# Moving the low parts of 60 weight blocks, the row gathers and half of the gates: a transformer kernel with product-key experts on one Trainium2 core

## The chip, the cores and the metric

The program runs on one core of a Trainium2 chip. The metric is the device time of one execution in microseconds. A core has five engines that run their own instruction streams in order and wait for each other through semaphores: TensorE (PE, matrix products, with its weight loads shown as PEld), VectorE (DVE), ScalarE (ACT), GpSimd (POOL) and SyncE (SP, which here issues most DMAs). Sixteen DMA engines move data; their requests come from SP's queue (q1 in the profile) and from POOL's (q0).

## What is computed

Two transformer blocks follow each other on one sequence of 512 tokens of width 1024, in float32. The first has differential attention, a pooling branch, a gated convolution and a gated feed-forward layer of width 2816. The second has three attention branches and then a feed-forward layer made of 16,384 experts, of which each token takes 128 (8 heads, 16 each). The change is about the last one, and about the feed-forward layer of the first block:

```python
def peer_ffn(h, w_q, keys1, keys2, u, v):
    q = (h @ w_q).reshape(B, S, PEER_HEADS, 2, half)
    s1 = jnp.einsum('bshd,hkd->bshk', q[..., 0, :], keys1)
    s2 = jnp.einsum('bshd,hkd->bshk', q[..., 1, :], keys2)
    v1, i1 = lax.top_k(s1, PEER_TOPK)
    v2, i2 = lax.top_k(s2, PEER_TOPK)
    cand = v1[..., :, None] + v2[..., None, :]           # 16 x 16 per head
    sv, si = lax.top_k(cand.reshape(..., 256), PEER_TOPK)
    e1 = jnp.take_along_axis(i1, si // PEER_TOPK, axis=-1)
    e2 = jnp.take_along_axis(i2, si % PEER_TOPK, axis=-1)
    experts, gates = e1 * N_KEYS + e2, jax.nn.softmax(sv, axis=-1)
    # per token: a = u[experts] . h ; out = (gelu(a) * gates) . v[experts]
```

## The kernel before

**Products in three parts.** A float32 product is made of three TensorE products: each operand is split into a high part (ScalarE copies it to float32r) and a low part (VectorE subtracts the high part from the whole), and high x high, low x high and high x low are added in PSUM (`product`, lines 394 to 396). Weights come in a fixed order as blocks of 128 x 1024 (512 KB). `Stream` loads a block on SP's queue into one of four raw buffers (`wr`), ScalarE makes `wh` (line 81) and, after `LAG` = 2 ticks, VectorE makes `wl` (line 83; through the counting wrapper `Counted` it shows as line 189). Three buffers of each are there, and up to two split blocks are kept ahead of the one in use.

**An order written out by hand.** Instructions are put in order by the Python program. After each three-part product (`gemm` calls it) comes a tick: `Later.tick` lets every waiting generator run its next step, and at last calls `fill`. `Balance` is the plan: a count of TensorE's columns (`pe`), and of VectorE's estimated work in the same unit (`dve`). `behind()` is the difference, and `room()` makes a generator wait while it is over 2000. A 384-column three-part product counts 3 x 396 = 1188, a VectorE instruction on 1024 float32 columns 2746. Nothing in the plan counts ScalarE or DMA.

**Stages.** The first block's feed-forward layer is three groups of w_gate_up and w_down blocks. Much later come the expert layer's stages:
- *Selection.* w_peer_q products and scores; `select` finds the top 16 on VectorE for three token groups of 128 (0 to 2) and, in a chain of its own, for the fourth (3).
- *u stage.* Tokens 0 to 383 (`ND`) go through all 16,384 experts as dense products: 128 u blocks, 24 TensorE instructions each. `ev_u` writes the Gelu of a block on ScalarE (line 1805) to one of two buffers `full`, and SP stores it in DRAM (`a_d`, 192 KB).
- *Gates.* Beside the u stage `gates` makes a dense gate matrix from the selection, in 48 groups of 8 tokens: VectorE makes two one-hot matrices (`oh1`, `oh2h`) and two products of one of them with the high and low part of the gate values (`ogh`), TensorE multiplies them (line 1709), ScalarE evicts to `stg` (line 1713), and SP stores in `g_d`.
- *v stage.* 128 v blocks. `fetch` reads Gelu and gate for eight blocks from DRAM into `ag`, `activate` multiplies them on VectorE, one block at a time and one block ahead, and splits the result (line 1797 and VectorE); lines 1863 to 1865 add all into eight PSUM banks.
- *Rows.* Tokens 384 to 511 take their own 128 experts each: 128 gathers of u rows and 128 of v rows (line 1642, an indirect DMA of 512 KB on POOL's queue into one of four buffers `ub`), each followed by one VectorE instruction of 1024 columns. `one_by_one` does one and asks for the gather four later. `fill` calls it at the end of a tick if `behind()` is under 800; v rows only in the v stage.

Of the kernel before, what the change touches and what calls it, by code (L numbers as in the profile page):

```python
# [22 lines left out]
D = 1024  # L23
# [21 lines left out]
NUB = 4  # L45


class Stream:
# [7 lines left out]
    def __init__(self, nc, raw, parts, entries, on_raw, later):  # L56
        self.nc, self.raw, self.parts, self.entries, self.on_raw = nc, raw, parts, entries, on_raw
        self.later = later
# [7 lines left out]
    def load(self):  # L66
        while self.loaded < len(self.entries) and self.loaded < self.done + self.RAW:
            key, ap, n, split = self.entries[self.loaded]
            t = self.raw.tile([128, 1024], F32, name="wr")
            self.nc.sync.dma_start(t[:, :n], ap)  # L70
            self.r[self.loaded] = t
            self.loaded += 1

    def _one(self):
# [14 lines left out]
        self.load()  # L89

# [68 lines left out]
class Balance:  # L159
# [3 lines left out]
    def __init__(self):  # L163
        self.pe = self.dve = 0.0
# [7 lines left out]
    def behind(self):  # L172
        return self.dve - self.pe

# [34 lines left out]
def tile_kernel(ctx, tc, a, out):  # L209
# [51 lines left out]
    ents(seq_ff, 1, range(40, 48))  # L261
# [11 lines left out]
    dr = ctx.enter_context(tc.tile_pool(name="dr", bufs=1, space=bass.MemoryType.DRAM))  # L273
    ph1 = ExitStack()
# [25 lines left out]
    stream = Stream(nc, wraw, wpart, entries, mod_chunk, later)  # L300
# [715 lines left out]
    with tc.tile_pool(name="ffp", bufs=2) as ffp:  # L1016
        for g, (f0, f1) in enumerate(FGROUPS):
# [444 lines left out]
    stream.low = dv  # L1462
    a_d = dr.tile([32, 128, 4, ND], F32, name="a_d")
# [89 lines left out]
    def select(t0, nt, big):  # L1553
# [5 lines left out]
        for h in HEADS:  # L1559
# [9 lines left out]
            cand, ixr, oneh = big()  # L1569
# [4 lines left out]
            for i in range(2):  # L1574
                for t in range(nt):
                    nc.scalar.activation(ixr[:, i, t], ixf[:, i, t, :, None].to_broadcast([128, 16, 16]), AF.Copy)
# [419 lines left out]
```

## Time and profile before

| | us |
|---|---|
| median of 3 runs | 2498.8 (2495.02 to 2503.24) |
| the profiled execution | 2499.26 |
| its span, first to last instruction | 2497.5 |
| TensorE busy in it | 2384.8 (95%) |
| VectorE busy | 1854.5 (74%) |
| ScalarE busy | 1081.7 (43%) |
| POOL busy | 456.4 (18%) |
| mean granted TensorE clock | 0.989 |

The page gives busy times and shares of the whole span, and then the span in 40 slices of 62 us. A share over the whole span is a mean over stages with different limits; so the table of stretches, the waits and the instructions in order of time are read for the places of interest. A tile's name in a row is that of the program (`wl<-wr,wh` is made from `wr` and `wh`); `x46` is a count. The feed-forward stage lies at about 390 to 700 us, the u stage at 1327 to 1938, the gates within it at 1585 to 1843, and the v stage at 1945 to 2488.

### The profile page before, as it was taken

The numbers are of one execution on the slowest core, as the hardware profiler recorded it, in microseconds if no ns is written. First come the engines' busy times: TensorE is split into PE (matmuls) and PEld (weight loads), VectorE is DVE, ScalarE is ACT, GpSimd is POOL, SyncE is SP. The second block draws the span as 40 slices with busy tenths as digits, with TensorE's granted clock in tenths as the row PEclk, the third lists the DMA queues.
The fourth block names the chain that finished last, engine by engine and source line by source line (L and its number), as shares of the span: only waits on it lengthen the run. The fifth ranks groups of instructions, "written<-read, shape, count | busy, mean of one in ns | idle before, by whom it ended". The sixth has DMA issues, their size and how long they took to land.

```text
span 2497.5 us, 35741 instructions
## 1 busy us (share of the span) xinstructions
PE 2384.8 (95%) x13075; PEld 2128.1 (85%) x13075; DVE 1854.5 (74%) x3722; ACT 1081.7 (43%) x1812; POOL 456.4 (18%) x434
## 2 busy tenths in 40 slices
PE   4899999999989999999999999999987899999998
PEld 2677788888868888777889999999987899999998
DVE  7678763333567776655699999988876889999994
ACT  3566332222445555533445444566642333333332
POOL 5310000000011100000000000111224444455440
PEclk9999999999999999999999999999998999999999
DMA  6973652222256643134325555689899999999993
GB/s 243 228 209 105 217 178 101 93 101 93 85 162 158 159 123 110 51 110 148 106 86 173 183 174 174 224 323 324 336 336 405 327 402 405 404 403 404 402 401 121
DMA packets 184511, 548.94 MB, mean 220 GB/s; under 512 B 22464, under 2 KB 59072, under 8 KB 183952
## 3 DMA queue, kind: packets, MB, share of 16 engines
q1 hardware_dynamic: 132720, 381.00, 42.7%
q0 software_dynamic: 51040, 165.04, 19.8%
q8 instruction: 103, 1.69, 0.3%
q14 instruction: 72, 0.59, 0.1%
q10 hardware_dynamic: 576, 0.62, 0.1%
HBM read 478.00 MB, written 68.71 MB: 219 GB/s over the span
## 4 chain that ended last, share of the span: by engine, by line
PE 77%; DMA 8%; issue 6%; DVE 5%; ACT 2%; POOL 1%; SPq 0%; DVEq 0%; ACTq 0%; POOLq 0%
PE pg L394 17%; PE pg L396 17%; PE pg L395 17%; PE pv L1864 6%; PE pv L1863 6%; PE pv L1865 6%; DMA a_d<-full 2%; DMA ub<-in_v,idx 2%; PE pt L602 1%; DMA ub<-in_u_rows,idx 1%; PE ps L1709 1%; DVE ada L297 1%; POOL ub L1642 1%; PE po L624 1%; DMA wr<-in_v 1%
## 5 line engine op out<-in xcount | busy, mean ns | idle before, releaser
L394 PE MATMUL pg<-hh,wh 128*128 128x512 f32 (+1 forms) x2088 | 792.4, 380 | 33.2 <-ACT full L1805 19.5
L395 PE MATMUL pg<-hl,wh 128*128 128x512 f32 (+1 forms) x2088 | 765.0, 366 | 9.2 <-POOL hl L508 8.9
L396 PE MATMUL pg<-hh,wl 128*128 128x512 f32 (+1 forms) x2088 | 765.6, 367 | 3.3 <-DVE wl L189 2.6
L81 ACT ACTIVATE wh<-wr 128x1024 fp32r<-128x1024 f32 (+2 forms) x446 | 465.7, 1045 | 411.7 <-PE pv L1864 268.2
L394 PEld LDWEIGHTS pg<-hh,wh 128*128 128x128 f32 x2088 | 397.2, 190 | 75.7 <-ACT full L1805 22.8
L396 PEld LDWEIGHTS pg<-hh,wl 128*128 128x128 f32 x2088 | 396.0, 190 | 48.8 <-DVE wl L189 3.6
L395 PEld LDWEIGHTS pg<-hl,wh 128*128 128x128 f32 x2088 | 397.3, 190 | 44.8 <-POOL hl L508 11.8
L189 DVE TENSOR_TENSOR wl<-wr,wh 128x1024 fp32r<-128x1024 f32 x270 | 329.6, 1221 | 90.1 <-ACT wh L81 89.2
L1863 PE MATMUL pv<-og,wh 128*128 128x384 f32 x1024 | 345.3, 337 | 7.0 <-ACT og L1797 7.0
L1864 PE MATMUL pv<-og,wh 128*128 128x384 f32 x1024 | 346.5, 338 | 3.0 <-DVE og L189 3.0
L1865 PE MATMUL pv<-og,wl 128*128 128x384 f32 x1024 | 345.1, 337 | 0.0
L83 DVE TENSOR_TENSOR wl<-wr,wh 128x1024 fp32r<-128x1024 f32 (+2 forms) x175 | 208.1, 1191 | 111.9 <-ACT wh L81 110.1
L1642 POOL DMA_INDIRECT ub<-in_u_rows,idx x128 | 151.1, 1180 | 706.5 <-DVE dots L189 514.2
L1642 POOL DMA_INDIRECT ub<-in_v,idx x128 | 183.1, 1431 | 179.6 <-DVE rows_o L189 161.8
L1863 PEld LDWEIGHTS pv<-og,wh 128*128 128x128 f32 x1024 | 192.9, 188 | 7.4 <-ACT og L1797 7.3
L1864 PEld LDWEIGHTS pv<-og,wh 128*128 128x128 f32 x1024 | 192.8, 188 | 6.7 <-DVE og L189 6.6
L1865 PEld LDWEIGHTS pv<-og,wl 128*128 128x128 f32 x1024 | 192.8, 188 | 0.0
L1805 ACT ACTIVATE full<-pg 128x384 f32<-128x384 f32 x128 | 63.0, 492 | 284.5 <-issue 142.6
L189 DVE CUSTOM_DVE_ANT_0 ub<-ub,rows_h 128x1024 f32<-128x1024 f32 x128 | 155.6, 1220 | 29.2 <-DMA ub<-in_u_rows,idx 29.1
L189 DVE SCALAR_TENSOR_TENSOR rows_o<-ub,dots,rows_o 128x1024 f32<-128x1024 f32 x127 | 162.4, 1279 | 11.9 <-DMA ub<-in_v,idx 11.5
L1713 ACT ACTIVATE stg<-ps 128x512 f32<-128x512 f32 x96 | 105.3, 1120 | 22.3 <-PE ps L1709 22.3
L1797 ACT ACTIVATE og<-ag 128x384 fp32r<-128x384 f32 x128 | 65.9, 515 | 32.5 <-DVE ag L189 28.7
(390 smaller groups left out, 3223.8 us busy)
## 6 DMA issues: line engine op xcount, KB each, us to landing
wr<-in_u SPq DMA_DIRECT2D x128, 512.0 KB, 4.7
wr<-in_v SPq DMA_DIRECT2D x128, 512.0 KB, 10.2
wr<-in_w_in SPq DMA_DIRECT2D x66, 512.0 KB, 3.4
a_d<-full SPq DMA_DIRECT2D x128, 192.0 KB, 3.4
g_d<-stg SPq DMA_DIRECT2D x32, 768.0 KB, 9.8
ag<-a_d SPq DMA_DIRECT2D x32, 768.0 KB, 9.6
ag<-g_d SPq DMA_DIRECT2D x32, 768.0 KB, 16.0
wr<-in_w_gate_up SPq DMA_DIRECT2D x44, 512.0 KB, 3.3
```

Source lines behind the costliest of these rows:

```text
L81: self.nc.scalar.activation(hi[:, :n], t[:, :n], AF.Copy)
L83: self.low.tensor_tensor(lo[:, :n], t[:, :n], hi[:, :n].bitcast(F32), op=OP.subtract)
L189: return f(*args, **kw)
L394: nc.tensor.matmul(ps[:m, :n], w[0][:, wk], rh, start=first, stop=False)
L395: nc.tensor.matmul(ps[:m, :n], w[0][:, wk], rl, start=False, stop=False)
L396: nc.tensor.matmul(ps[:m, :n], w[1][:, wk], rh, start=False, stop=last)
L1642: nc.gpsimd.indirect_dma_start(out=got[n], out_offset=None, in_=flat[what], in_offset=bass.IndirectOffsetOnAxis(ap=idx[:, s:s + 1], axis=0))
L1713: nc.scalar.activation(stg[:, :, k0:k0 + 4].rearrange("p e t -> p t e"), pg.rearrange("p (t e) -> p t e", t=4), AF.Copy, scale=1.0 / GS)
L1797: nc.scalar.activation(hi, la, AF.Copy)
L1863: nc.tensor.matmul(ps, wh[:, c], hi, start=b == 0, stop=False)
L1864: nc.tensor.matmul(ps, wh[:, c], lo, start=False, stop=False)
L1865: nc.tensor.matmul(ps, wl[:, c], hi, start=False, stop=b == 127)
```

## The change

- **Low parts.** While the feed-forward stage runs, entries `("pre", k)` for u blocks 0 to 59 are put between its weights: the block is loaded, split, and its low part is written to DRAM (`made`) on POOL's queue. In the u stage the low part of these blocks is loaded from there on POOL's queue instead of made on VectorE.
- **Rows.** The plan also counts DMA (`transfer`, `queued`). `fill` may take a row with up to 4000 behind while fewer than 0.95 rows per block since their start are done, and none with over 5000 units of DMA queued; in the v stage rows are spread evenly over 124 blocks.
- **Gates.** The product with the low part of the gate values goes from VectorE to ScalarE, one token (128 columns, every second element) at a time.
- **Blocks two at a time.** `activate` gates two blocks in one go, two blocks ahead; the first two are gated before the u stage is over; fetches come two blocks earlier.
- **Smaller ones.** The last sums of `select` are a tree of additions; `LAG` is 4 in the expert stages; every third Gelu has a buffer of its own (`au`).

```diff
@@ -43,6 +43,8 @@
+NPRE = 60
+RATE = 0.95
...
@@ -68,6 +70,7 @@
+            self.bal.transfer(n)
...
@@ -79,14 +82,31 @@
             self.nc.scalar.activation(hi[:, :n], t[:, :n], AF.Copy)
+            if not self.ready_made(key, lo):
+                yield self.LAG
+                self.low.tensor_tensor(lo[:, :n], t[:, :n], hi[:, :n].bitcast(F32), op=OP.subtract)
+            self.p[i] = (hi, lo)
+        elif key[0] == "pre":
+            hi = self.spare.tile([128, 1024], F32R, name="ph")
+            lo = self.spare.tile([128, 1024], F32R, name="pl")
+            self.nc.scalar.activation(hi, t, AF.Copy)
             yield self.LAG
-            self.low.tensor_tensor(lo[:, :n], t[:, :n], hi[:, :n].bitcast(F32), op=OP.subtract)
-            self.p[i] = (hi, lo)
+            self.low.tensor_tensor(lo, t, hi.bitcast(F32), op=OP.subtract)
+            yield 1
+            self.nc.gpsimd.dma_start(self.made[key[1]], lo)
         else:
...
         self.load()
+    def ready_made(self, key, lo):
+        if key[0] != "u" or key[1] >= NPRE:
+            return False
+        self.nc.gpsimd.dma_start(lo, self.made[key[1]])
+        self.bal.transfer(D)
+        return True
...
@@ -171,6 +191,13 @@
+    def transfer(self, n):
+        self.dma = max(self.dma, self.pe) + 2.88 * n
+    def queued(self):
+        return self.dma - self.pe
...
@@ -237,12 +264,14 @@
-    def ents(seq, every=None, extra=()):
+    def ents(seq, every=None, extra=(), ahead=0):
...
+            if 0 <= k - 4 < ahead:
+                entries.append((("pre", k - 4), a["u"][k - 4], D, False))
...
@@ -258,7 +287,7 @@
-    ents(seq_ff, 1, range(40, 48))
+    ents(seq_ff, 1, range(40, 48), NPRE)
...
@@ -1460,6 +1493,7 @@
+    stream.LAG = 4
...
@@ -1584,16 +1618,20 @@
+            dv.tensor_tensor(oneh, sab.rearrange("p i t k -> p (i t) k")[:, :, None, :].to_broadcast(
+                [128, 2 * nt, 16, 16]), iota16[:, None].to_broadcast([128, 2 * nt, 16, 16]), op=OP.is_equal)
+            yield from room()
...
-                dv.tensor_tensor(oneh[i], sab[:, i, :, None, :].to_broadcast(sq4),
-                                 iota16[:, None].to_broadcast(sq4), op=OP.is_equal)
+                part = oneh[:, nt * i:nt * i + nt]
+                dv.tensor_tensor(part, part, ixr[i], op=OP.mult)
...
-            for i in range(2):
-                dv.tensor_tensor(oneh[i], oneh[i], ixr[:, i], op=OP.mult)
+            for n in (8, 4, 2):
+                dv.tensor_tensor(oneh[:, :, :n], oneh[:, :, :n], oneh[:, :, n:2 * n], op=OP.add)
...
-                dv.reduce_sum(dst[:, ts, h, :], oneh[i].rearrange("p t j k -> p t k j"), axis=AX)
-                yield from room()
+                dv.tensor_tensor(dst[:, ts, h, :], oneh[:, nt * i:nt * i + nt, 0], oneh[:, nt * i:nt * i + nt, 1],
+                                 op=OP.add)
+            yield from room()
...
@@ -1689,7 +1725,12 @@
         stage["pe"] = bal.pe
-        if bal.behind() < 800:
+        soon = "out" not in stage and stage["at"] < RATE * (stage.get("blk", 0) - stage.get("go", 0))
+        if "out" in stage:
+            first = stage.setdefault("first", stage["at"])
+            if stage["at"] > first + (stage["blk"] + 1) * (len(jobs) - first) / 124:
+                return
+        if bal.behind() < (4000 if soon else 800) and bal.queued() < 5000:
             one_by_one()
...
@@ -1743,9 +1784,13 @@
-            for r in range(2):
-                dv.tensor_tensor(og[:, r], oh1, of(gp[:, r, tk]), op=OP.mult)
-                yield from room()
+            dv.tensor_tensor(og[:, 0], oh1, of(gp[:, tk]), op=OP.mult)
+            yield from room()
+            for n in range(TG):
+                nc.scalar.activation(og[:, 1, n // 2, :, n % 2], oh1[:, n // 2, :, n % 2], AF.Copy,
+                                     scale=gT[:, tk.start + n:tk.start + n + 1])
+                if n % 4 == 3:
+                    yield 1
...
@@ -1760,11 +1805,13 @@
+            bal.transfer(32 * NG)
...
+            later.spawn(activate(0), 2)
...
@@ -1787,23 +1836,30 @@
             t = AG[b // 8]
-            la = t[:, 0, b % 8]
-            lav = la.rearrange("p (s t) -> p s t", s=8)
-            lg = t[:, 1, :, NG * (b % 8):NG * (b % 8) + NG]
+            two = [128, 2, ND]
+            la = t[:, 0, b % 8:b % 8 + 2]
+            lav = la.rearrange("p b (s t) -> p b s t", t=NG)
+            lg = t[:, 1, :, NG * (b % 8):NG * (b % 8) + 2 * NG].rearrange("p s (b t) -> p b s t", t=NG)
             dv.tensor_tensor(lav, lav, lg, op=OP.mult)
             yield 2
-            parts = w3.tile([128, 2048], BF, name="og").bitcast(F32R)
-            hi, lo = parts[:, :ND], parts[:, 512:512 + ND]
+            if b % 4:
+                parts = hp.tile([128, 4, ND], F32R, name="parts", tag="hl")
+                hi, lo = parts[:, :2], parts[:, 2:]
+            else:
+                hi, lo = (w3.tile([128, 1024], F32R, name="part", tag="og")[:, :2 * ND].rearrange(
+                    "p (b t) -> p b t", b=2) for i in range(2))
             nc.scalar.activation(hi, la, AF.Copy)
-            yield 2
+            yield 3
             dv.tensor_tensor(lo, la, hi.bitcast(F32), op=OP.subtract)
-            AC[b] = (hi, lo)
+            for i in range(2):
+                AC[b + i] = hi[:, i], lo[:, i]
...
         def f(ps):
-            t = tmp.tile([128, 512], F32, name="full")[:, :ND]
+            t = w3.tile([128, ND], F32, name="au", bufs=1) if b % 3 == 2 else tmp.tile([128, 512], F32, name="full")[:, :ND]
             nc.scalar.activation(t, ps, AF.Gelu)
             nc.sync.dma_start(a_d[b // 4, :, b % 4], t)
+            bal.transfer(ND)
         return f
...
@@ -1848,13 +1904,13 @@
     rows_o = hp.tile([128, 4, KD, 128], F32, name="rows_o", tag="hh")[:, 0]
-    stage["out"] = rows_o
-    for _ in activate(0):
-        pass
+    stage.update(out=rows_o, blk=0)
     for b in range(128):
-        if b % 8 == 7:
+        stage["blk"] = b
+        if b % 8 == 5:
             later.spawn(fetch(b // 8 + 2))
-        later.spawn(activate(b + 1))
+        if b % 2 == 0:
+            later.spawn(activate(b + 2))
         wh, wl = stream.get(("v", b))
```

## Rows read from the trace of the kernel before

**Rows 1.** The page's 40 slices of the span, busy tenths of TensorE.

```profile
PE   4899999999989999999999999999987899999998
```

**Rows 2.** Stretches: us, each engine's busy us (count), PEclk, DMA share, GB/s.

```profile
390.00:700.00 310.00, 309.37 (x1357) 251.40 (x1356) 123.06 (x137) 89.36 (x114) 0.54 (x1) 1.00 0.28 95
1358.00:1585.00 227.00, 227.00 (x1311) 226.77 (x1310) 215.06 (x672) 95.53 (x157) 7.34 (x6) 1.00 0.55 187
1585.00:1843.00 258.00, 258.00 (x1965) 242.84 (x1964) 227.95 (x328) 171.24 (x198) 46.88 (x43) 1.00 0.87 312
1843.00:1945.00 102.00, 72.95 (x363) 68.81 (x361) 63.35 (x92) 22.44 (x32) 45.05 (x38) 0.91 1.01 394
1945.00:2440.00 495.00, 491.79 (x2798) 488.00 (x2799) 452.69 (x571) 178.10 (x236) 234.93 (x170) 1.00 1.01 394
```

**Rows 3.** ScalarE in order of time, end of u: start, us, what, idle before.

```profile
1847.62 0.49 ACT L1805 ACTIVATE full<-pg 128x384 f32<-128x384 f32 x1 [2.72 <-issue]
1848.01 1.05 ACT L81 ACTIVATE wh<-wr 128x1024 fp32r<-128x1024 f32 x1
1851.78 0.49 ACT L1805 ACTIVATE full<-pg 128x384 f32<-128x384 f32 x1 [2.72 <-PE pg L396]
1861.93 0.49 ACT L1805 ACTIVATE full<-pg 128x384 f32<-128x384 f32 x1 [8.72 <-DMA a_d<-full]
...
1940.89 0.49 ACT L1805 ACTIVATE full<-pg 128x384 f32<-128x384 f32 x1 [0.32 <-DMA a_d<-full]
```

**Rows 4.** ScalarE's waits 1845 to 1946: total us, times, longest.

```profile
ACT full L1805 <- DMA a_d<-full: 70.4, 13, 9.0
```

**Rows 5.** DMA issues, KB, median us to landing: 1840:1945; last row 1600:1840.

```profile
wr<-in_u SPq DMA_DIRECT2D x10, 512.0 KB, 9.5
a_d<-full SPq DMA_DIRECT2D x16, 192.0 KB, 11.2
ub<-in_u_rows,idx POOLq DMA_INDIRECT x38, 8.3
...
wr<-in_u SPq DMA_DIRECT2D x46, 512.0 KB, 6.2
```

**Rows 6.** VectorE's groups from 1945 on: busy us, mean ns, idle before.

```profile
L189 DVE CUSTOM_DVE_ANT_0 ub<-ub,rows_h 128x1024 f32<-128x1024 f32 x45 | 54.8, 1218 | 1.4 <-DMA ub<-in_u_rows,idx 1.4
```

**Rows 7.** Lines 1805 and 1863: ns min/median/max, first and last start.

```profile
L1805 ACT ACTIVATE full<-pg x128: 491/492/550, 1327.4 to 1940.9; 128x384 f32<-128x384 f32 x128
...
L1863 PE MATMUL pv<-og,wh x1024: 332/337/687, 1945.2 to 2487.9; 128*128 128x384 f32 x171
```

**Rows 8.** TensorE's waits from 1945 on.

```profile
PE pv L1863 <- ACT og L1797: 7.0, 1, 7.0
PE pv L1864 <- DVE og L189: 3.0, 5, 1.2
```

**Rows 9.** POOL in order of time: the fourth gather.

```profile
1379.94 1.65 POOL L1642 DMA_INDIRECT ub<-in_u_rows,idx  x1 [16.80 <-DVE tif L189]
```

**Rows 10.** VectorE's groups 1600 to 1840.

```profile
L189 DVE TENSOR_TENSOR ogh<-oh,gp 128x1024 f16<-128x1024 f16 x88 | 56.9, 687 | 1.1
L189 DVE TENSOR_TENSOR wl<-wr,wh 128x1024 fp32r<-128x1024 f32 x46 | 56.3, 1223 | 16.5 <-ACT wh L81 16.1 <-DMA a_d<-full 0.3
```

**Rows 11.** ScalarE in order of time: four scaled copies, six copies, evictions.

```profile
1313.29 1.15 ACT L1525 ACTIVATE scs<-ps,rt 128x128 f32<-128x128 f32 x4
...
1380.51 1.93 ACT L1576 ACTIVATE og<-tif 128x256 bf16<-128x256 f32 x6
...
1838.98 1.07 ACT L81 ACTIVATE wh<-wr 128x1024 fp32r<-128x1024 f32 x1
1839.95 3.04 ACT L1713 ACTIVATE stg<-ps 128x512 f32<-128x512 f32 x3
```

**Rows 12.** Line 1642: ns min/median/max.

```profile
L1642 POOL DMA_INDIRECT ub<-in_u_rows,idx x128: 932/1012/1759, 1358.8 to 2065.4; - x128
```

**Rows 13.** VectorE's groups 1358 to 1585.

```profile
L189 DVE TENSOR_REDUCE e2f<-oh 128x48 f32<-128x768 bf16 x8 | 13.1, 1639 | 0.0
```

More of the change, by code (lines that the diff above doesn't have):

```diff
@@ L54, with __init__ @@
     LAG = 2
-    def __init__(self, nc, raw, parts, entries, on_raw, later):
+    def __init__(self, nc, raw, parts, entries, on_raw, later, bal):
         self.nc, self.raw, self.parts, self.entries, self.on_raw = nc, raw, parts, entries, on_raw
-        self.later = later
+        self.later, self.bal = later, bal
         self.low = nc.vector
@@ L163, in __init__ @@
     def __init__(self):
-        self.pe = self.dve = 0.0
+        self.pe = self.dve = self.dma = 0.0
     def product(self, n):
@@ L273, in tile_kernel @@
     dr = ctx.enter_context(tc.tile_pool(name="dr", bufs=1, space=bass.MemoryType.DRAM))
+    made = dr.tile([NPRE, 128, D], F32R, name="made")
     ph1 = ExitStack()
@@ L298, in mod_chunk @@
                                        mod[:, j:j + 1])
-    stream = Stream(nc, wraw, wpart, entries, mod_chunk, later)
+    stream = Stream(nc, wraw, wpart, entries, mod_chunk, later, bal)
+    stream.made = made
     def load_ada(k):
@@ L1551, in top16, with select @@
         yield 0
-    def select(t0, nt, big):
+    def select(t0, nt, places):
         sq4 = [128, nt, 16, 16]
@@ L1575, in select @@
                 for t in range(nt):
-                    nc.scalar.activation(ixr[:, i, t], ixf[:, i, t, :, None].to_broadcast([128, 16, 16]), AF.Copy)
+                    nc.scalar.activation(ixr[i][:, t], ixf[:, i, t, :, None].to_broadcast([128, 16, 16]), AF.Copy)
             si = w3.tile([128, nt, 16], U32, name="si" + x)
@@ L1611, in select, with places3, places1 @@
         yield from room()
-    def places3():
-        cand = w3.tile([128, 2048], BF, name="og")[:, :1536].bitcast(F32).rearrange(
-            "p (t a b) -> p t a b", t=3, a=16)
-        ixr = w3.tile([128, 2048], BF, name="og")[:, :1536].rearrange(
-            "p (i t a b) -> p i t a b", i=2, t=3, a=16)
-        oneh = [w3.tile([128, 1024], BF, name="oh2")[:, :768].rearrange("p (t a b) -> p t a b", t=3, a=16)
-                for i in range(2)]
+    def places3(nt):
+        cand = w3.tile([128, 2048], BF, name="og")[:, :512 * nt].bitcast(F32).rearrange(
+            "p (t a b) -> p t a b", t=nt, a=16)
+        ixr = [w3.tile([128, 1024], BF, name="oh2")[:, :256 * nt].rearrange("p (t a b) -> p t a b", t=nt, a=16)
+               for i in range(2)]
+        oneh = w3.tile([128, 2048], BF, name="og")[:, :512 * nt].rearrange("p (t a b) -> p t a b", t=2 * nt, a=16)
         return cand, ixr, oneh
-    def places1():
+    def places1(nt):
         def part(c, n, **kw):
-            return small[:, 256 * c:256 * (c + n)]
-        cand = part(0, 2).bitcast(F32).rearrange("p (t a b) -> p t a b", t=1, a=16)
-        ixr = part(2, 2).rearrange("p (i t a b) -> p i t a b", i=2, t=1, a=16)
-        oneh = [part(4 + i, 1).rearrange("p (t a b) -> p t a b", t=1, a=16) for i in range(2)]
-        return cand, ixr, oneh
+            return small[:, 256 * c:256 * (c + n)].rearrange("p (t a b) -> p t a b", a=16, **kw)
+        cand = small[:, :512].bitcast(F32).rearrange("p (t a b) -> p t a b", t=1, a=16)
+        return cand, [part(2 + i, 1, t=1) for i in range(2)], part(4, 2, t=2)
     idx = c3.tile([128, 128], I32, name="idx")
@@ L1665, in rows_in @@
         yield 20
-        stage["go"] = True
+        stage["go"] = stage.get("blk", 0)
     def one_by_one():
@@ L1782, in fetch @@
                     "s p b t -> p s (b t)"))
+                bal.transfer(4 * ND)
                 yield P["f1"]
```

11 lines of the change are left out of this document (7 added, 4 removed).

## The prediction

> **What bounds the kernel now.** I read the 40 slices first [rows 1]: TensorE is at nine tenths or more almost everywhere, and the one dip in the second half lies at 1850 to 1950 us. The table of stretches [rows 2] says why the rest cannot give much: from 1358 to 1843 TensorE is busy all the time, although VectorE stands at 88 to 95% there, so a lighter VectorE alone buys nothing in that stretch. From 1843 to 1945 TensorE is busy 73 of 102 us while the DMA engines are at 1.01 and move 394 GB/s.
>
> ScalarE's instructions at that place [rows 3] show the mechanism. Undisturbed, the Gelu of one u block follows the last by 4.16 us. After 1851.8 us the gaps grow to as much as 10 us, and the waits give the reason [rows 4]: 13 Gelus wait 70.4 us in total for `a_d<-full`, the store that must free their output buffer. Those stores take 11.2 us to land there, a u load 9.5 and a gathered row block 8.3, against 6.2 for a u load between 1600 and 1840 [rows 5]. The cause is a burst: `fill` gathers a row only when the plan (`Balance`, which counts columns while the program is put in order) has VectorE under 800 behind, which hardly happens before selection and gates are over, so most of the rows come at once at the end of u. Even so 45 of the 128 u rows are left for the v stage [rows 6].
>
> What that costs: 13 blocks end between 1851.8 and the end of u. TensorE's first v product starts at 1945.2 [rows 7] after a wait of 7.0 us [rows 8], so u ended at 1938.2. That is 86.4 us for 13 x 4.16 = 54.1 us of work: **32.3 us lost, and 7.0 more at the crossing** (the wait there is for the first gated block, whose VectorE work stands behind row products). The v stage runs from 1945.2 to about 2488 [rows 7], 543 us, where 128 x 4.16 = 532.5 would be u's pace: at most 10 us, of which waits show 3.0 [rows 8].
>
> **The change, part by part.** Times are against the profiled execution, 2499.3 us (span 2497.5); the median of the runs shown is 2498.8, so the difference is nothing.
>
> *Rows on a schedule.* In the plan a row may now be taken at up to 4000 behind while fewer than 0.95 per block are done, if less than 5000 units of DMA are queued. 2.88 units per column make a 512 KB load 2949; u's 24 products make a block 9504 units, in 4.16 us. So the plan's DMA rate is 524288 bytes x 9504 / 2949 / 4.16 us = 406 GB/s, what the saturated stretches move (394, [rows 2]). The queue can then be some 8000 units (3.5 us) long, not a pile of 13 late stores. The first Gelu of u is at 1327.4 us [rows 7] and the fourth gather goes at 1379.9 [rows 9], some 13 blocks on, so rows can run from about block 13. Before block 60 a block moves u, low part and store, 2949 + 2949 + 1106 = 7004 units (columns x 2.88), which leaves (9504 - 7004) / 2949 = 0.85 rows per block: 40 rows by block 60. At 0.95 that makes 86 by block 108, and then (9504 - 2949 - 1106 - 1860 for the first two gate fetches) / 2949 = 1.2 per block: about 110 at the end of u against 83 now. What is late next is the v stage with 18 + 128 rows in place of 173: (146 + 128) x 0.524 MB + 128 x 0.393 MB = 194 MB (the second term is the gate and Gelu blocks) in 539 us, 360 GB/s, below the 394 of now. I take back 30 of the 32.3 us. The crossing: block 0 is gated inside the u stage by `activate(0)`, before the end; I take 6 of 7.0. In v, gating two blocks ahead removes the 3.0 and the lower load a little more: 4.
>
> *Third buffer for the Gelu output.* One block more of patience for a store; counted in the 30.
>
> *Low parts ahead of time.* In u, 60 VectorE subtractions of 1.22 us (the row `wl<-wr,wh` of [rows 10]) go, 73 us. That is worth nothing directly, as TensorE had no wait there. It pays for the rows, which cost as much per block: the gates begin about where they began. In the feed-forward stage 60 conversions (1.07 us on ScalarE, [rows 11]) and 60 subtractions are added to 310 us in which VectorE is busy 123 and ScalarE 89 [rows 2]: 196 and 152. Its DMA goes from 95 to about 285 GB/s. At 312 GB/s TensorE is busy all of 1585 to 1843 and a u load lands in 6.2 us, and here a product takes 310 us / 1357 x 24 = 5.5 us, uses up two loads, and has four buffers of them, so a weight is asked for some 8 us ahead. Cost 0 at best; at worst one conversion and one subtraction (2.3 us) stand ahead of the last activation of each of the three feed-forward groups, 7 us. I take 1.
>
> Each low part is fetched on POOL's queue when the block three before it has released its buffer, and is needed two blocks later, 8.3 us. POOL takes about 1 us for a gather [rows 12] and the landing is 6.2 us by the u loads of the busy stretch: 7.2, in time. By the 8.3 us of the jam it would be 9.3, 1 us late per two blocks, 0.5 x 47 blocks = 24 us. Behind a waiting fetch stand gathers only, which have four buffers. The schedule keeps the queue short, so I am near the first end: 2 us.
>
> *Gates' second half to ScalarE.* This is the cost I fear. Per group VectorE loses one of four 0.69 us products [rows 10], and ScalarE gets eight scaled copies of 128 columns: 384 in all. Four copies of 128 columns with a per-partition scale take 1.15 us, and six of 256 take 1.93 [rows 11]: 0.29 each, 111 us. From 1585 to 1843, all 48 groups and, at 46 blocks in 240 us [rows 10], 49 blocks, ScalarE is busy 171 of 258 us [rows 2]. 171 + 111 = 282, 24 more than there is. Back to back they overlap: Gelu to conversion is 0.39 [rows 3], conversion to eviction 0.97, three evictions 3.04 or 0.96 apart [rows 11]. So 49 x 1.36 + 96 x 0.96 + 111 = 270, 12 more than TensorE's 258. It counts only if the plan, which knows nothing of ScalarE, keeps the pace. Now a group needs 6 ticks by its yields and waits (room under 2000 behind, 1188 per tick); with 46 blocks for 44 groups [rows 10] it took 8.4, the rest going to splits and rows. The new group has 3 plus 4 ticks, and 4 of these let VectorE catch up: 7 plus some 1.5 makes 8.5, the same pace. Who waits is TensorE, for ScalarE's products and evictions, and VectorE, as the single `oh1` buffer is now released by ScalarE. Between 12 and 24, I take **15 us lost**. From below: nothing, if groups spread over 4 blocks more. From above: between copies of 256 columns (0.32) and conversions of 1024 (0.97) a column costs 0.85 ns, and the evictions, which write scattered, take 0.96 for 512, about twice that per column. The new copies step over every second element; if that doubles their columns too, a copy costs 0.29 + 0.11 = 0.40, all of them 154 us, and 159 + 154 - 258 = 55 us are lost. I keep the lower price, as 4 bytes of step are nearer to contiguous rows than the evictions' 192.
>
> [...]
>
> *Selection by a tree of additions*: two reductions of 1.63 us per head [rows 13] become four shorter passes, some 2 us per head, 15 us of VectorE that no one on the path waits for: 0.
>
> **The sum**: -30 - 6 - 4 + 15 + 1 + 2 = -22, and 2499.3 - 22 = **2477 us**. Its own range, with ScalarE at 5 to 27 and the others at their bounds, is 2465 to 2492.
>
> **Rivals.** *ScalarE is not the bound* (the groups spread out, or copies overlap down to 0.2 us): all that is lost now comes back, 2462, down to 2456 if the v stage gives all its 10. For it: TensorE has 4 us of patience per eviction. Against: 270 of 258.
>
> *Slower: ScalarE at the scattered price* in the gate stage: 55 in place of 15, 2477 + 40 = 2517. It turns the sign from 0.354 us per copy on, where 159 + 384 x 0.354 - 258 = 37 us eat all that is won. For it: the evictions' row, and that TensorE waits in order behind every late product. Against: the step is 4 bytes, not 192.
>
> *The jam moves forward*: from block 13 to 60 the DMA demand is 419 GB/s (1.74 MB per 4.16 us), above the 394, and low parts come late: 24 us, 2499, no change. For it: saturated landings of 8.3 us. Against: the plan's queue limit. A second way to the same lateness is POOL itself: beside a busy VectorE its gathers take 0.93 to 1.76 us [rows 12], so a hold of 0.8 us is seen, which alone is still in time (8.0 of 8.3). [...]
>
> *It doesn't do what it says*: the plan still holds rows back to the end, and the burst stays: 2499 + 15 - 10 = 2504.
>
> **How the numbers follow.** Forecast 0.50, no ScalarE bound 0.21, slower 0.13, jam forward 0.12, burst stays 0.04. About 0.3% (7.5 us) is what a measurement here can tell. Faster: 0.47 of the forecast, 0.21, and 0.06 of the jam, 0.74. Same: 0.03 + 0.04 + 0.03 + 0.02 = 0.12. Slower: 0.13 + 0.01 = 0.14. The range 2455 to 2507 takes in the forecast, the first and third rival and leaves out the scattered price.
>
> **What would show it.** Gelus 4.16 us apart to the end of u, no wait on `a_d<-full`, about 110 u rows done by then; v starting within 1 us; v at under 390 GB/s. ScalarE over 95% busy in the gate stage and TensorE under 97%, waiting on `full` or on ScalarE's `og`. Wrong would be: `wl` waits on `made` in the first 60 blocks, gaps in the feed-forward stage, a copy far from 0.29 us.

## The result and the profile after

The changed kernel takes 2470.3 us (median of 4 runs, 2465.6 to 2472.1), the kernel before 2499.3 (4 runs, 2495.0 to 2503.2): a ratio of 0.9887, with a 95% interval of 0.987 to 0.9905. The profiled executions have spans of 2463.7 and 2497.5 us. The 33.8 us between them lie here:

| stretch | before | after | difference |
|---|---|---|---|
| start to the first Gelu of u | 1327.4 | 1322.3 | -5.1 |
| first Gelu of u to the first v product | 617.8 | 599.3 | **-18.5** |
| v products | 543.4 | 533.4 | **-10.0** |
| tail | 8.9 | 8.7 | -0.2 |

The first line is not the change. It arises between about 720 and 765 us, in instructions that both kernels share, and varies from one execution to the next: the first Gelu of u came at 1321.8 to 1330.5 us in the twelve runs below. So the stretches, not the medians, settle differences of a few microseconds.

The slices of the page, TensorE's row, answer [rows 1]; the dip in the second half is gone:

```profile
PE   4899999999998999999999999999999999999998
```

The table of stretches of after answers [rows 2] (us; each engine's busy us and count, in the order PE, PEld, DVE, ACT, POOL; PEclk, DMA share, GB/s). The fourth is the gate stage, the fifth the end of u, the sixth v:

```profile
390.00:700.00 310.00, 308.38 (x1350) 250.47 (x1348) 179.61 (x189) 139.39 (x165) 27.72 (x53) 1.00 0.85 273
1380.00:1420.00 40.00, 35.16 (x189) 34.84 (x189) 33.90 (x130) 12.97 (x22) 9.79 (x15) 0.91 0.90 330
1420.00:1551.00 131.00, 131.00 (x750) 129.03 (x749) 105.41 (x407) 57.40 (x98) 47.26 (x57) 1.00 1.06 404
1551.00:1824.00 273.00, 267.44 (x1994) 250.10 (x1993) 214.29 (x304) 267.90 (x584) 64.33 (x57) 1.00 0.92 329
1843.00:1921.60 78.60, 77.04 (x442) 76.08 (x440) 47.63 (x63) 27.05 (x39) 28.37 (x21) 1.00 1.02 396
1921.60:2455.00 533.40, 533.37 (x3074) 533.34 (x3075) 437.53 (x418) 180.35 (x190) 184.74 (x142) 1.00 0.93 347
```

The end of u moves as many bytes a second as the jam did (396 GB/s against 394), but TensorE is busy 77.0 of 78.6 us in place of 73 of 102: the rate alone does not stall it. What the limit on queued DMA does is shown by the run without it below: TensorE busy 79.9 of 100 us at 371 GB/s. The next fence has waits of after for a store to free its Gelu buffer, which answer [rows 4] (engine, tile, line, releaser: total us, times, longest; 70.4 us there), and TensorE's waits, which answer [rows 8]. The last row is the wait of the first v product.

```profile
ACT au L1860 <- DMA a_d<-au: 2.9, 1, 2.9
...
PE pg L428 <- DMA wl<-made: 5.2, 2, 4.8
PE ps L1750 <- ACT stg L1754: 2.8, 5, 1.3
PE ps L1750 <- ACT ogh L1790: 1.2, 1, 1.2
PE pg L426 <- ACT full L1860: 0.7, 1, 0.7
...
PE pv L1919 <- issue: 0.6, 1, 0.6
```

VectorE's row products from 1921 us on answer [rows 6]: 18 u rows are left for v where 45 were, so 110 are done.

```profile
L216 DVE CUSTOM_DVE_ANT_0 ub<-ub,rows_h 128x1024 f32<-128x1024 f32 x18 | 21.8, 1220 | 3.0 <-DMA ub<-in_u_rows,idx 2.9
```

The Gelus of one buffer, v products and the scaled copies by line (ns min/median/max, first and last start) answer [rows 7]:

```profile
L1860 ACT ACTIVATE full<-pg x86: 469/492/660, 1322.3 to 1921.1; 128x384 f32<-128x384 f32 x86
...
L1919 PE MATMUL pv<-part,wh x512: 332/336/443, 1921.6 to 2446.0; 128*128 128x384 f32 x171
...
L1790 ACT ACTIVATE ogh<-oh,gT x384: 417/430/567, 1551.2 to 1821.2; 128x128 f16<-128x128 f16 x192
```

**The gate stage** is now ScalarE's. In order of time (start, us, instruction; no idle time between them), one of its cycles:

```profile
1624.38 0.53 ACT L1860 ACTIVATE full<-pg 128x384 f32<-128x384 f32 x1
1624.82 1.04 ACT L84 ACTIVATE wh<-wr 128x1024 fp32r<-128x1024 f32 x1
1625.76 2.47 ACT L1790 ACTIVATE ogh<-oh,gT 128x128 f16<-128x128 f16 x8
1628.10 1.99 ACT L1754 ACTIVATE stg<-ps 128x512 f32<-128x512 f32 x2
1629.89 0.52 ACT L1860 ACTIVATE au<-pg 128x384 f32<-128x384 f32 x1
```

Eight copies take 2.34 us to the next instruction, 0.29 each. A Gelu follows the last after 5.51 us here. TensorE did 46 u blocks and 44 groups in 240 us in [rows 10], so a group takes it (240 - 46 x 4.16) / 44 = 1.1 us, and a block with a group 5.3.

**The one late low part.** POOL in order of time, and the product that waited:

```profile
1375.06 1.06 POOL L1677 DMA_INDIRECT ub<-in_u_rows,idx  x1 [0.30 <-issue]
1376.42 0.98 POOL L1677 DMA_INDIRECT ub<-in_u_rows,idx  x1 [0.30 <-issue]
1377.70 0.93 POOL L1677 DMA_INDIRECT ub<-in_u_rows,idx  x1 [0.30 <-issue]
1378.94 0.93 POOL L1677 DMA_INDIRECT ub<-in_u_rows,idx  x1 [0.30 <-issue]
1379.87 0.60 POOL L107 DMA_DIRECT2D wl<-made  x1
...
1391.60 0.69 PE L428 MATMUL pg<-hh,wl 128*128 128x384 f32 x1 [4.84 <-DMA wl<-made]
```

The four gathers that start the rows go out in one piece, 2 MB, and the low part is queued behind them. It is asked for at 1379.9 and used 11.7 us later, after a wait of 4.8.

### The profile page after: what moved, and what is told of

Same layout as the page of the kernel before. It is cut to its first block, busy times and chain, and to the rows that moved or that the text cites. A ratio compares the mean times of both kernels' runs of the same rounds, so it can differ in the third digit from the quotient of the medians.

```text
span 2463.7 us, 36298 instructions
## 1 busy us (share of the span) xinstructions
PE 2373.1 (96%) x13075; PEld 2120.1 (86%) x13075; DVE 1808.5 (73%) x3578; ACT 1225.1 (50%) x2192; POOL 506.5 (21%) x554
## 4 chain that ended last, share of the span: by engine, by line
PE 77%; ACT 8%; issue 6%; DVE 4%; DMA 4%; POOL 1%; SPq 0%; DVEq 0%; ACTq 0%; POOLq 0%
PE pg L426 16%; PE pg L428 16%; PE pg L427 16%; PE pv L1919 7%; PE pv L1921 7%; PE pv L1920 7%; ACT ogh L1790 3%; ACT stg L1754 2%; ACT wh L84 1%; PE pt L634 1%; DVE ada L327 1%; DMA wl<-made 1%; PE po L656 1%; PE ps L1750 1%; PE po L560 1%
## 5 line engine op out<-in xcount | busy, mean ns | idle before, releaser
L216 DVE TENSOR_TENSOR wl<-wr,wh 128x1024 fp32r<-128x1024 f32 x210 | 257.0, 1224 | 133.3 <-ACT wh L84 132.5
L1677 POOL DMA_INDIRECT ub<-in_v,idx x128 | 162.9, 1273 | 293.9 <-DVE rows_o L216 273.2
L1677 POOL DMA_INDIRECT ub<-in_u_rows,idx x128 | 156.7, 1224 | 309.0 <-DVE dots L216 290.0
L1919 PE MATMUL pv<-part,wh 128*128 128x384 f32 x512 | 172.0, 336 | 0.6 <-issue 0.6
L1921 PE MATMUL pv<-part,wl 128*128 128x384 f32 x512 | 172.1, 336 | 0.0
L1920 PE MATMUL pv<-part,wh 128*128 128x384 f32 x512 | 171.9, 336 | 0.0
L1919 PE MATMUL pv<-parts,wh 128*128 128x384 f32 x512 | 171.5, 335 | 0.0
L1920 PE MATMUL pv<-parts,wh 128*128 128x384 f32 x512 | 171.4, 335 | 0.0
L1921 PE MATMUL pv<-parts,wl 128*128 128x384 f32 x512 | 171.2, 334 | 0.0
L1790 ACT ACTIVATE ogh<-oh,gT 128x128 f16<-128x128 f16 x384 | 120.1, 450 | 2.3 <-DVE oh L216 2.3
L94 DVE TENSOR_TENSOR pl<-wr,ph 128x1024 fp32r<-128x1024 f32 x60 | 73.3, 1222 | 50.7 <-ACT ph L92 50.7
L1860 ACT ACTIVATE full<-pg 128x384 f32<-128x384 f32 x86 | 44.2, 514 | 122.1 <-issue 87.0
```

The source lines that it names most:

```text
L94: self.low.tensor_tensor(lo, t, hi.bitcast(F32), op=OP.subtract)
L216: return f(*args, **kw)
L1677: nc.gpsimd.indirect_dma_start(out=got[n], out_offset=None, in_=flat[what], in_offset=bass.IndirectOffsetOnAxis(ap=idx[:, s:s + 1], axis=0))
L1790: nc.scalar.activation(og[:, 1, n // 2, :, n % 2], oh1[:, n // 2, :, n % 2], AF.Copy, scale=gT[:, tk.start + n:tk.start + n + 1])
L1919: nc.tensor.matmul(ps, wh[:, c], hi, start=b == 0, stop=False)
L1920: nc.tensor.matmul(ps, wh[:, c], lo, start=False, stop=False)
```

## The experiments

**The theory** is the sum of the prediction: the schedule takes the jam out of the end of u; the gates' second half makes ScalarE the bound of the gate stage, some 15 us; low parts arrive in time; v gains little. **The rivals**: ScalarE isn't the bound; the schedule, its queue limit or the low parts are not what helps; the low parts' lateness is a matter of DMA load, not of one burst; the gain in v is the rows' or the DMA's rather than that of gating two blocks at a time. All diffs are against the changed kernel. "The u stretch" is from the first Gelu of u to the first v product.

**The changed kernel again**, as a measure for the others.

> The changed kernel once more, beside the experiments, so that they can be compared with it on one chip. Every theory expects 2465 to 2474 us. It also tells whether the 5 us that its profiled execution gained before the u stage (first Gelu of u at 1322.3 us, 1327.4 before), where nothing was changed, come again: if they belong to the change the first Gelu is again within 1 us of 1322, if they are chance it may lie anywhere from 1320 to 1330.

2465.6 us (2461.8 to 2470.4), a ratio to before of 0.9867 (0.9841 to 0.9893). u stretch 599.3 and v 533.4, each as in the first profile to 0.1 us: the stretches repeat where medians scatter. The first Gelu of u came at 1323.3 us, 1 us from the 1322.3 of the first profile, which settles nothing by itself; the other eleven runs below, which share the instructions ahead of it, spread over 1321.8 to 1330.5, so the 5 us are put down to chance.

### Is ScalarE the bound of the gate stage?

```diff
...
-            dv.tensor_tensor(og[:, 0], oh1, of(gp[:, tk]), op=OP.mult)
-            yield from room()
-            for n in range(TG):
-                nc.scalar.activation(og[:, 1, n // 2, :, n % 2], oh1[:, n // 2, :, n % 2], AF.Copy,
-                                     scale=gT[:, tk.start + n:tk.start + n + 1])
-                if n % 4 == 3:
-                    yield 1
+            for r in range(2):
+                dv.tensor_tensor(og[:, r], oh1, of(gp[:, r, tk]), op=OP.mult)
+                yield from room()
```

The lines left out keep the low part of the gate values beside the high part in `gp`, as before the change.

> The changed kernel with one part undone: the product of the one-hot matrix with the low part of the gate values is made by VectorE again, as before, all else kept. Theory A (ScalarE is the bound of the gate stage and costs 14 us: 273 us for 48 groups and 50 blocks, where TensorE needs 50 x 4.16 + 48 x 1.06 = 259): ScalarE falls to about 70% of the gate stage, a cycle of one block and one group goes from 5.5 us to 5.2, and the time falls by 8 to 14 us, to 2457 to 2463. Theory B (VectorE is the scarcer engine, so that the work pays for itself on ScalarE): VectorE has 4 x 0.69 + 1.22 + 1.1 = 5.1 us per 5.2 us cycle, groups and rows crowd each other, the gate stage gets longer or rows are left for the end of u, and the time stays or rises by up to 15 us.

2456.6 us (2454.4 to 2457.4), ratio 0.9829 (0.9805 to 0.9852). The u stretch is 589.6, 9.7 less.

The second kernel does this in every other group and leaves the rest on ScalarE:

> The changed kernel with this product on VectorE for every second group and on ScalarE for the others. Theory A (ScalarE bound, 14 us): ScalarE needs 1.36 + 1.8 + 1.18 = 4.3 us per cycle of 5.2, TensorE is the bound again, and the time falls by 10 to 14 us, to 2456 to 2460. Theory B (VectorE is the scarcer one): VectorE has 4.75 us of 5.2, the gain is smaller than half of that, 2464 to 2470.

2457.6 us (2455.9 to 2462.1), ratio 0.9836 (0.9811 to 0.986); u stretch 587.7, 11.6 less. One stretch of the gate stage, first of the kernel with the product on VectorE, then of the one with half:

```profile
1550.00:1800.00 250.00, 250.00 (x1834) 237.35 (x1833) 218.25 (x319) 157.78 (x184) 66.45 (x55) 1.00 0.93 337
```
```profile
1550.00:1800.00 250.00, 250.00 (x1845) 236.98 (x1844) 207.46 (x305) 203.01 (x356) 68.82 (x56) 1.00 0.94 340
```

TensorE is busy 250 of 250 us in both, with VectorE at 83 to 87% and ScalarE at 63 to 81%. So ScalarE was the bound, and moving the product there lost some 10 us; VectorE had room for it. By the medians the two are the same, 8 to 9 us under the changed kernel in the same comparison (by the stretch 9.7 and 11.6).

### The four first gathers

```diff
         for n in range(NUB):
             gather(n)
-        yield 20
+            yield 8
```

> The changed kernel with the first four gathers one block apart (8 ticks after each) instead of in one go and 20 ticks at the end. Theory C (the one wait of TensorE for a low part, 4.8 us at 1391.6 us with some 4 us at half clock after it, comes from four gathers of 512 KB that stood ahead of the fetch on POOL's queue): no wait for a low part over 1 us, granted clock 1.00 between 1380 and 1420 us, and 5 to 8 us less, 2462 to 2465. Theory D (the fetch was late because the DMA engines are saturated from there on, by whatever): the wait stays somewhere in the first 60 blocks and the time with it, 2468 to 2472.

2464.8 us (2462.4 to 2468.3), ratio 0.9865 (0.984 to 0.989): by the median no different from the changed kernel. But the u stretch is 593.3, 6.0 less; in this profile 4.3 of that were lost before u, in the part that varies. The stretch that answers the second stretch of after, and TensorE's wait for low parts from 1320 us on:

```profile
1380.00:1420.00 40.00, 40.00 (x232) 40.00 (x231) 39.38 (x169) 17.41 (x31) 14.60 (x19) 1.00 1.03 388
```
```profile
PE pg L428 <- DMA wl<-made: 1.2, 4, 0.4
```

232 products where there were 189, at more DMA load (388 GB/s against 330) and no wait over 0.4 us. So the lateness came from the burst on POOL's queue, not from the load. That it gives back 6.0 and not 4.0 (5.2 less 1.2) goes with the granted clock behind the wait, in the changed kernel:

```profile
1392.00:1396.00 4.00, 4.00 (x14) 4.00 (x14) 3.96 (x20) 0.00 (x0) 0.00 (x0) 0.50 0.66 252
1396.00:1400.00 4.00, 4.00 (x23) 4.00 (x22) 4.00 (x22) 1.44 (x2) 1.36 (x2) 0.91 0.19 16
1400.00:1404.00 4.00, 4.00 (x25) 4.00 (x24) 2.81 (x18) 1.44 (x2) 1.37 (x3) 1.00 0.89 321
```

At a granted clock of 0.50 14 products fall into 4 us, those at its edges counted, at 1.00 25. The products behind the wait start 0.32 us apart in place of 0.17, for some 2.4 us more in all. A busy time of 4.00 in all three stretches shows nothing of it; the counts do.

### Schedule, queue limit, low parts: which of them takes the jam away?

The old rule for taking a row, so that the pace and the queue limit both go (the even spread in v is kept):

```diff
-        if bal.behind() < (4000 if soon else 800) and bal.queued() < 5000:
+        if bal.behind() < 800:
```

> The changed kernel with one part undone: in fill a row is taken only with VectorE under 800 behind, and no look is taken at the DMA queue, as before (the even spread in the v stage is kept). Theory A (the schedule is what removed the jam): the rows come when selection is over, with fewer VectorE subtractions in the way even faster than before, over 1 row per block beside the gates; the DMA queue runs 30 us and more behind, stores of Gelu blocks and low parts come late, TensorE waits for them, and 20 to 35 us are lost: 2488 to 2505. Theory B (a lighter VectorE alone spreads the rows): no such waits, 2465 to 2475.

2518.7 us (2517.4 to 2520.5), ratio 1.0074 (1.0052 to 1.0095). u stretch 652.2, v 533.4. No row is done before 1498 us (1389 in the changed kernel), and then some 1.6 per block. The stretch around the end of u, and TensorE's waits from 1320 us on:

```profile
1750.00:1950.00 200.00, 166.17 (x939) 157.83 (x938) 134.39 (x192) 85.02 (x154) 86.42 (x67) 0.93 0.96 360
```
```profile
PE pg L428 <- DVE wl L216: 26.6, 12, 5.3
...
PE pg L428 <- DMA wl<-made: 13.0, 9, 4.1
```

No low parts from the feed-forward stage, the schedule kept:

```diff
-NPRE = 60
+NPRE = 0
```

> The changed kernel without the low parts made ahead (none of the 60; VectorE makes all in the u stage, nothing is added to the feed-forward stage), rows on the schedule, all else kept. Theory A (the subtractions taken from VectorE pay for the rows, which now run beside the selection): VectorE has selection, a subtraction and a row per block until selection is over, the gates begin some 30 blocks later, near block 78, and end with u; what follows them (last store, first fetch, first gated block, some 30 us) stands with TensorE idle: 2490 to 2505. Theory B (the low parts only fill spare time and the schedule alone does it): 2462 to 2475, less the 5 us that the first fetches cost.

2514.2 us (2512.0 to 2517.8), ratio 1.0056 (1.0039 to 1.0073). u stretch 638.9, v 536.3. VectorE now has the rows and the low parts at once, and the gates run from 1685.6 to 1942.6 us in place of 1551 to 1824, so the first gated block is late. The stretch there, and TensorE's two waits from 1320 us on:

```profile
1850.00:1950.00 100.00, 72.79 (x536) 63.70 (x535) 71.47 (x107) 92.19 (x209) 25.21 (x21) 0.77 0.81 295
```
```profile
PE pv L1919 <- ACT part L1851: 25.1, 1, 25.1
PE ps L1750 <- ACT stg L1754: 18.7, 13, 1.8
```

No look at the queued DMA, all else kept:

```diff
-        if bal.behind() < (4000 if soon else 800) and bal.queued() < 5000:
+        if bal.behind() < (4000 if soon else 800):
```

> The changed kernel without the limit on queued DMA in fill (rows at 0.95 per block and up to 4000 behind are kept; more where VectorE is under 800 behind). Theory A (the limit keeps the DMA queue short): between the end of selection and the end of u the queue grows to 17 to 28 us twice, and TensorE waits for low parts, loads or stores: 10 to 25 us lost, 2477 to 2492. Theory B (the pace of 0.95 is enough): 2464 to 2470.

2504.9 us (2502.6 to 2513.0), ratio 1.003 (1.0015 to 1.0044). u stretch 635.3, v 533.4. All 128 u rows are done before the end of u, and the jam is back:

```profile
1850.00:1950.00 100.00, 79.90 (x413) 76.89 (x412) 55.24 (x76) 25.26 (x36) 36.18 (x28) 0.91 0.96 371
```
```profile
PE pg L428 <- DVE wl L216: 11.4, 6, 2.9
PE pg L428 <- DMA wl<-made: 10.0, 4, 4.6
...
PE pg L426 <- ACT full L1860: 6.0, 1, 6.0
```

Each of the three ends 0.3 to 0.7% slower than the kernel before, and 9 to 14 us beyond the range that was expected of it. The changed kernel's own costs are still in them: about 10 us of ScalarE in the gate stage, and some 6 for the late low part where there are low parts. So they show what a part is worth within the changed kernel, by the growth of its u stretch: 36.0 us without the limit, 52.9 without limit and pace, 39.6 without the low parts. Without low parts VectorE can't carry the rows; with low parts but without pace and limit the rows come in a heap; and with the pace but without the limit the queue jams all the same. The pace was not taken out with the limit kept, and what one of them gives alone on the kernel before was not tried.

### Where do the microseconds in v come from?

One block gated at a time and one ahead, in the buffers and with the fetches of before the change:

```diff
-            la = t[:, 0, b % 8:b % 8 + 2]
+            la = t[:, 0, b % 8]
...
-        if b % 2 == 0:
-            later.spawn(activate(b + 2))
+        later.spawn(activate(b + 1))
...
```

> The changed kernel with blocks gated one at a time and one ahead, in the buffers and with the fetches of before (the first block is still gated before u ends). The v stage took 543 us before and takes 533.4 now. Theory A (the shorter look-ahead and its buffers cost it): v takes 540 to 543 again, the products stand 0.1744 us apart where they now stand 0.1735, and the time rises by 7 to 10 us. Theory B (the DMA engines at 404 GB/s did it, which the even spread of the rows took down to 357): v stays at 533 to 535 us.

2469.2 us (2466.6 to 2474.8), ratio 0.987 (0.9849 to 0.9892). u stretch 599.6, v 539.4, 6.0 more. All of it lies at the crossing, where the second block isn't there; neither theory put it there, and the pace of the products, which the first expected to be slower, is 0.1733 us. TensorE's wait, and the first two stretches of v; the granted clock reads 0.77 in the first, and 48 products start in 15.1 us, where at 0.1735 us each there would be 87, so 39 x 0.1735 = 6.8 us are lost. In the next stretch nothing is:

```profile
PE pv L1913 <- DVE og L216: 3.6, 1, 3.6
```
```profile
1924.90:1940.00 15.10, 11.49 (x48) 11.18 (x49) 11.65 (x18) 3.02 (x4) 6.16 (x6) 0.77 0.96 340
1940.00:1960.00 20.00, 20.00 (x118) 20.00 (x117) 16.07 (x25) 7.37 (x10) 6.03 (x6) 1.00 0.75 243
```

v rows taken as soon as VectorE is under 800 behind, not spread, and without the limit in v:

```diff
-            if stage["at"] > first + (stage["blk"] + 1) * (len(jobs) - first) / 124:
-                return
-        if bal.behind() < (4000 if soon else 800) and bal.queued() < 5000:
+        if bal.behind() < (4000 if soon else 800) and ("out" in stage or bal.queued() < 5000):
```

> The changed kernel with the rows of the v stage taken whenever VectorE is under 800 behind, with no spread and no look at the DMA queue there, as before. Theory A (139 rows, of which 128 are v rows, are few enough: the v stage is held by TensorE, and the spread buys nothing): v stays at 533 to 535 us, the DMA engines move 404 GB/s in its first three quarters. Theory B (the spread is what freed the v stage): loads of v come late, v takes 538 to 545 us.

2499.7 us (2489.3 to 2505.1), ratio 1.0011 (0.9997 to 1.0026); the profiled execution is the shortest of them. v takes 560 us, 26.6 more, which is beyond both theories. A stretch of v, the waits of TensorE in v, and one of ScalarE:

```profile
1950.00:2250.00 300.00, 285.88 (x1607) 278.77 (x1606) 266.92 (x249) 95.12 (x101) 167.03 (x107) 0.99 1.02 395
```
```profile
PE pv L1918 <- DVE parts L216: 12.9, 11, 2.0
...
ACT wh L84 <- DMA wr<-in_v: 40.6, 10, 5.5
```

So v is not free without spread and limit. With the spread but without the limit it took 533.4 us in two runs above (there with no u rows left for v), which points to the spread. The kernel before moved as much (394 GB/s in [rows 2]) and lost less in v; why is not settled.

### The third Gelu buffer

```diff
-            t = w3.tile([128, ND], F32, name="au", bufs=1) if b % 3 == 2 else tmp.tile([128, 512], F32, name="full")[:, :ND]
+            t = tmp.tile([128, 512], F32, name="full")[:, :ND]
```

> The changed kernel with two Gelu output buffers in place of three. Theory A (the queue limit alone ends the waits for stores; the third buffer is spare): ScalarE waits for a store at most twice, 2464 to 2470. Theory B (with the DMA engines near full the third buffer carries part of the gain): 5 to 30 us of waits of ScalarE for a_d at the end of u, 2472 to 2485.

2473.5 us (2468.9 to 2476.6), ratio 0.9902 (0.988 to 0.9924). u stretch 602.4, 3.1 more; v 534.9. ScalarE's wait for a store is back, but spread out:

```profile
ACT full L1860 <- DMA a_d<-full: 92.0, 36, 4.3
...
PE pv L1919 <- ACT full L1860: 3.3, 1, 3.3
```

92 us in 36 waits of up to 4.3 cost 3.1 in the stretch; in [rows 4] 70.4 in 13 of up to 9.0 went with 32 lost. Waits of ScalarE of about one u block's time (4.16 us) are mostly not passed on to TensorE. The second row shows one that is: the first v product waits 3.3 us for the last Gelu, where it waited 0.6.

### The two repairs together

Half of the gates' product on VectorE and the gathers apart, and then all of it on VectorE and the gathers apart:

> Two edits together: the low gate product on VectorE for every second group, and the first four gathers one block apart. If the two losses (ScalarE in the gate stage, 11.6 us from the first Gelu of u to the first v product; the one late low part, 6.0 us) are separate, that stretch falls from 599.3 us to 582, near the 579 that TensorE needs, and the time to some 2450. If the later start of the rows moves work into the gate stage, the sum is smaller: 586 us or more, 2455 to 2460.

> The low gate product on VectorE for all groups, and the first four gathers one block apart. If the two losses are separate, 599.3 - 9.7 - 6.0 = 583.6 us from the first Gelu of u to the first v product and some 2451 us. VectorE is the fullest of the three kernels here (87% in the gate stage); if that is too much once the rows start later, 590 us, 2457.

2456.1 us (2453.6 to 2460.4), ratio 0.9832 (0.9815 to 0.985), and 2457.8 (2456.3 to 2462.3), ratio 0.9842 (0.9825 to 0.986). The u stretches are 583.9 and 584.9: 15.4 and 14.4 less than the changed kernel, nearly the 17.6 and 15.7 that the single repairs add up to. The medians show no more than the first repair by itself; the first Gelu of u came at 1328.4 and 1328.5 in these two profiles, 6 later than in after's. Half on VectorE with the gathers apart is the best by its median, but the kernel with all of the product on VectorE is 0.4 us behind it, in another comparison, well within their scatter. Either beats both kernels of the case.

## Why the prediction was right, point by point

**The sum.** -22 was forecast; -29 came in the medians and -33.8 in the profiles, of which 5.1 lie before u and are put down to chance and 0.2 in the tail. u and v together gave -28.5.

**Rows on a schedule (-30) and the crossing (-6): right.** 42 u rows were done by block 60, 89 by block 108 and 110 at the end of u, where 40, 86 and about 110 were forecast; v began after 0.6 us, where 7.0 were lost; the waits for `a_d<-full` are gone. Of the u stretch's -18.5, the gates took +9.8 and the late low part +6.0 (both below); with -6.4 at the crossing, -28 is left for the schedule. That is a remainder, not a measurement; that it is lost without the low parts, without the limit, and without limit and pace together, is measured.

**Gates to ScalarE (+15): right in kind, some 5 too dear.** From 1551 to 1800 us ScalarE did 46 Gelus and 44 groups. By the prediction's durations that is 46 x 1.36 + 88 x 0.96 + 352 x 0.29 = 249 us, and the stretch is 249 (85 of the 88 evictions fall into it, so the two agree to some 3 us). TensorE needed 240 for the same 46 and 44 in [rows 10]. So 9 us are lost, 9.8 for all 48 groups, and undoing the edit gave 9.7 and 11.6. The stage as a whole says the same: from the last Gelu before its first product to the first Gelu after its last eviction both kernels do 51 blocks and 48 groups, in 264.1 us before and 274.1 after. The step that failed is the choice of 15 between 12 and 24, and the 258 against which the 12 was set: the evenly paced part [rows 10] was the better measure. The sign on TensorE was wrong too: it shows as 98% busy (267.4 of 273), not under 97%, with only 4.0 us of waits for ScalarE. A loss of 4%, spread over many short gaps, doesn't show in TensorE's busy time. ScalarE's 98% shows it, and so do the weight loads: busy 94% of the gate stage in [rows 2], 92% after, and 95% with the product back on VectorE.

The price of a copy turned the sign in a rival: 0.29 us held (2.34 for eight), not 0.40.

**Low parts (feed-forward +1, fetches +2): right, but for one event.** TensorE is busy 308.4 of 310 us in the feed-forward stage at 273 GB/s (about 285 forecast, though its own terms, 60 times 1.05 MB in 310 us beside the 95 GB/s, give 298; 52 of the 60 stores fall into the stretch), and the last write of `xT`, behind that stage, comes 0.8 us later than before. The fetches cost some 6.0, not 2, by what spacing the gathers gave back. The prediction spoke of the queue behind a waiting fetch, and of the landing time; it did not ask what stands ahead of a fetch. Four gathers do, once. The rival that the jam moves forward did not come: from 1420 to 1551 us the DMA moves 404 GB/s and TensorE is busy 131.0 of 131. Its second way, fetches slowed on POOL itself, was not seen either: every fetch of a low part took 0.53 to 0.60 us on POOL, the one that was late among them, though the gathers of u rows took 0.93 to 2.00; what makes a gather longer was not shown.

**v (-4): the mechanism was right, the size was not: -10.0.** The step that failed is "waits show 3.0". That was TensorE's own wait row [rows 8]. The row of its weight loads, in the same view of the kernel before, is more than double, and products in order of time show what a stall costs, and what the crossing leaves behind:

```profile
PEld pv L1864 <- DVE og L189: 6.6, 13, 1.5
```
```profile
1948.83 0.52 PE L1864 MATMUL pv<-og,wh 128*128 128x384 f32 x1
1949.15 0.52 PE L1865 MATMUL pv<-og,wl 128*128 128x384 f32 x1
...
2292.47 0.33 PE L1863 MATMUL pv<-og,wh 128*128 128x384 f32 x1
2293.99 0.44 PE L1864 MATMUL pv<-og,wh 128*128 128x384 f32 x1 [1.19 <-DVE og L189]
2294.27 0.34 PE L1865 MATMUL pv<-og,wl 128*128 128x384 f32 x1
```

The wait reads 1.19, but the product starts 1.52 after the last one, 1.35 more than the 0.17 between undisturbed products, and the next is late by another 0.11. All such intervals of over 0.25 us after the crossing cost 5.8 us before and 0.1 after. Twelve more, of mostly 0.32, stand right behind the 7.0 us wait at 1945, where the granted clock reads 0.50 up to 1949: 2.2 us. A further 2.5 come from the last 755 products before, which follow at 0.1766 us where the others follow at 0.1733; after, it is 0.1735 throughout, which takes 0.5 back. 2.2 + 5.7 + 2.5 - 0.5 = 9.9, of 10.0 between the first and the last v product. The slower pace of the last products begins at about 2350 us, the granted clock reads 1.00, and it goes on when the DMA has almost ended (73 GB/s from 2440 on). ScalarE's conversions take 1.06 us ahead of that time and behind it, so not every engine slows. The cause stays open, and no trace of the changed kernel or of the other runs shows such a pace. Of the rest, gating two at a time takes away a second stall at the crossing, worth 6.0 in the changed kernel, and the even spread of the rows takes away the later ones: the run with single blocks and the spread has none.

**The selection (0).** Nothing in the u stretch asks for another value, but it was not tried by itself, and neither was `LAG`.

So the total was right for its reasons, with three terms off: the gates 5 too dear, the fetches 4 too cheap, v 6.0 too small. That they add up to only 7 us is in part luck, as the fetches go against the other two.

## What to carry to other kernels

When the last jam comes from work that the plan puts off, look at three things together: which engine has room for it earlier, a pace for it, and a limit on what it may queue; here leaving out the early work or the limit, or limit and pace together, made the kernel slower than it was before the change. Work taken off a loaded engine must be priced on the engine that gets it, in the stage where it lands and with all that is already there: ScalarE's durations from the old trace gave the length of the new stage. And read a stall from the starts of the products and from the weight loads' waits, not from the engine's own wait row or its busy share.

## What the runs showed of the hardware

- DMA at 404 GB/s (share 1.06) for 131 us left TensorE busy all the time, while 394 GB/s in [rows 2] went with 29 us of idle time in 102. The rate did not tell what came late here; the transfers queued ahead did: spacing four gathers took away a wait of 4.8 us at more load, and dropping the queue limit brought the jam back at 371 GB/s.
- Behind one wait of 4.8 us, after a stretch in which TensorE was busy 59.7 of 59.7 us, the granted clock read 0.50: 14 products in the 4 us behind it, against 25 in 4 us at 1.00.
- ScalarE copies that step 4 bytes cost what contiguous ones do in [rows 11], 0.29 us per 128 columns back to back, while its evictions with a step of 192 bytes stay at 0.9 to 1.0 us per 512.
